# Two SwiGLU feed-forward layers of a hybrid encoder, their products rewritten as Strassen's seven

## The chip, the cores and the metric

The kernel runs on one core of one Trainium2 chip. The metric is the device time of one execution in microseconds (us), lower is better. TensorE multiplies, VectorE (DVE), ScalarE (ACT) and GpSimd (POOL) do the elementwise work, and SyncE (SP) issues every DMA of the program.

## The reference

Two layers work on 1024 tokens of 1024 channels in float32. Layer 0 mixes by a convolution and a recurrence, layer 1 by differential attention, and each is followed by a feed-forward part. `D_FF` is 2816, that is 22 tiles of 128 columns.

```python
def swiglu(x, w_gate, w_up, w_down):
    return (jax.nn.silu(x @ w_gate) * (x @ w_up)) @ w_down
...
for layer in range(DEPTH):            # 2
    y = conv_lru_mixer(...) if layer % 2 == 0 else diff_attention_mixer(...)
    x = layer_norm(DN_ALPHA * x + y, mix_ln_g[layer], mix_ln_b[layer])
    x = layer_norm(DN_ALPHA * x + swiglu(x, ffn_w_gate[layer], ffn_w_up[layer], ffn_w_down[layer]),
                   ffn_ln_g[layer], ffn_ln_b[layer])
```

## The kernel before

SBUF is 35 pages of 128x1024 float32 (`g`, given out by `alloc`, from the front of a queue into which released pages go at the end) beside two tiles `xt` that hold the transposed activations x^T. A page may be cut into two half pages (`halloc`). PSUM is eight banks of 128x512.

Every product is in the format float32r, on operands that are split first: `split` copies a number's high part with ScalarE and takes the rest with a VectorE subtraction whose two inputs are both in SBUF (or one in PSUM). `three` then issues three matmuls for one product of 128 x 128 by 128 x 512: high by high, high by low, low by high. So each tile product costs three matmuls of 512 columns, and each operand costs one ScalarE and one VectorE instruction.

The tokens are worked on in two halves, A (tokens 0 to 511) and B. In the feed-forward part a chunk is two column tiles: `ff_up` takes for each of them the gate's and the up projection's weights ("units", 128x1024, loaded and split whole) against the eight 128-row tiles of x^T, 24 matmuls for each of the two weights and each half; `ff_down` multiplies the chunk's activations, which stay in SBUF, with two units of the down projection, 48 matmuls for a half, into PSUM, and adds each bank to the residual page with a VectorE instruction. A chunk of one half is so 96 + 48 = 144 matmuls. The first chunks of half A (`ffn_lead`) are run earlier, beside other work, as cover: four of them (`lead0`) beside the VectorE-heavy convolution of half B in layer 0, ten (`lead1`) beside and after the attention of half B in layer 1. `mix` interleaves these: for each unit of time of the attention's products it lets `ratio2` = 1.5 units of feed-forward products run. `turn` transposes a half of x on TensorE, in 128x128 pieces, into `xt`.

The order of the instructions on each engine is not the order of the code. Class `Order` records every instruction and what it touches, prices each by a table of engine times, and gives each engine a list order by latest start; the order is fixed when the program is built. Every instruction is issued through one helper, so that nearly all rows of the profile carry one line, L378. They are told apart by engine, operation, tiles and shape.

Of the kernel before, what the change touches and what calls it, by code (L numbers as in the profile page):

```python
# [37 lines left out]
class _Fake:  # L38
    """Stands for every object of the tracer in the pass that only records the order of the units."""
# [20 lines left out]
class Page:  # L60
    """[128, 1024] of SBUF, or [128, 512]: a half of one of these or of a k tile of x^T."""
# [10 lines left out]
class Unit:  # L72
    """[128, 1024] of a weight: loaded, then split."""
# [9 lines left out]
class Order:  # L83
    """Records what the trace issues and what it touches, and gives each engine an order for it: of the
    instructions whose data is there, the one that the later ones wait for most urgently, on a model of the
    engines' times.  Only the order is taken from the model; Tile still derives every wait from the data."""
# [12 lines left out]
    # ------------------------------------------------------------- recording  # L99
# [83 lines left out]
    def price(self, eng, name, out, reads, a, k):  # L183
# [14 lines left out]
        if eng == "act":  # L198
            f = a[2] if name == "activation" else None
            fn = str(f).split(".")[-1] if f is not None else "Copy"  # L200
            src = reads[0]
# [29 lines left out]
    # ------------------------------------------------------------ scheduling  # L231
    def lag(self, p, o, raw):
        """time from the end of op p to the earliest start of op o, which depends on it."""
        if p.dma:
            return 1070 if o.eng == "pe" else 910
        if p.eng == o.eng:
            return (127 if p.eng == "dve" else 100 if p.eng in ("act", "pool") else 0) if raw else 0
        return {"pe": 197, "act": 140, "dve": 130, "pool": 75, "sp": 0}[p.eng] + (self.margin if o.eng == "pe" else 0)

    def solve(self):  # L240
# [6 lines left out]
        # latest starts, with the products back to back in the order of the trace  # L247
# [28 lines left out]
        # list scheduling  # L276
# [73 lines left out]
    def apply(self):  # L350
# [4 lines left out]
        # a page goes to its next user only when the one before has had it  # L355
# [29 lines left out]
class Core:  # L385
    """The engines, with every call recorded."""
# [6 lines left out]
# the order of layer 0's steps, up to the output projection of half A; the letters are those of layer0_in  # L393
# [3 lines left out]
class Trunk:  # L397
    def __init__(self, tc, io, order=None, lead0=4, lead1=10, ratio1=1.65, ratio2=1.5, pool_a=(13, 13, 12, 8), pool_b=9,
# [19 lines left out]
        self.ahead = 1  # L418

    # ---------------------------------------------------------------- memory  # L420
    def setup(self, sb, ps, dr):
# [8 lines left out]
        self.r_d = dr.tile([HALF, D], F32, name="r_d")  # L430
        self.SM = sb.tile([P, NSMALL], F32, name="SM")
# [10 lines left out]
        self.ring_x = deque()  # L442
        self.banks = deque(range(8))
# [6 lines left out]
    def ring(self, name, n, bufs):  # L450
        """n small columns out of a ring of bufs."""
# [13 lines left out]
    def halloc(self, r=False):  # L465
        """half a page, from a ring of these that takes in and gives back whole pages."""
# [7 lines left out]
    def pair(self):  # L474
        """[128, 2, 512]: half B of two k tiles of x^T while that holds nothing, or a page."""
        return self.ring_x.popleft() if self.ring_x else self.alloc(True)
# [5 lines left out]
    def part(self, p, b):  # L482
        """half b of a pair, or a half page."""
        return self.pr(p) if p.kind == "h" else self.two(p, True)[:, b, :]

    def lend(self):
        """half B of x^T as pages."""
        for i in range(8):
            t = (self.XTH, self.XTL)[i // 4][:, 2 * (i % 4):2 * (i % 4) + 2, HALF:]
            self.ring_x.append(Page(t, True, "x", i))  # L490

    def release(self, *pages):
        for p in pages:
            if p.kind == "g":
                self.free.append(p.idx)
            elif p.kind == "x":
                self.ring_x.append(p)
# [23 lines left out]
    # ----------------------------------------------------------------- units  # L521
# [7 lines left out]
    def load(self, key):  # L529
        u = Unit(self.alloc())  # L530
        src = self.unit_src(key)
        # the first units come in pieces, so that the products start with the first of these
# [14 lines left out]
    def split(self, hi, lo, src):  # L547
        """hi + lo = src exactly (24 bits), each in a form that float32r carries."""
# [3 lines left out]
    def prefetch(self, n=9999):  # L552
        """Loads ahead, as far as pages are free; three pages are kept for each unit until it is split."""
        if self.dry:
            return
        while (self.next_load < min(n, len(self.order)) and self.live < self.cap
# [35 lines left out]
    # ------------------------------------------------------------- products  # L592
    def three(self, out, ah, al, bh, bl, start, stop):
        """out += (ah + al)^T (bh + bl), without the product of the two low parts."""
# [5 lines left out]
    def colmul(self, bank, u, h):  # L600
        """bank[128 columns, 512 tokens] = unit^T x^T for half h."""
# [15 lines left out]
    # ----------------------------------------------------------- layer norm  # L617
# [5 lines left out]
    def layer_norm(self, r, g, b, spread=False, store=None, parts=1):  # L623
        """in place; the last steps are spread over ScalarE and GpSimd or done in parts, each stored at once."""
# [19 lines left out]
    def transpose_in(self, src, t):  # L644
        """x^T of token tile t, split, into XT."""
# [12 lines left out]
    # ------------------------------------------------------------ constants  # L658
    def constants(self):
# [11 lines left out]
        # per-channel vectors  # L671
# [8 lines left out]
    def mixer_constants(self):  # L680
        nc, io = self.nc, self.io
        # -8 softplus(-lambda), with softplus(y) = max(y, 0) + log1p(exp(-|y|)) and
        # log1p(e) = 2 atanh(e / (2 + e)) as a series that converges to float32 for e in [0, 1]
# [20 lines left out]
        # block-diagonal gate weights  # L704
# [11 lines left out]
    # -------------------------------------------------------------- layer 0  # L716
# [13 lines left out]
    def glu(self, i, h, bv, bg):  # L730
        """val * sigmoid(gate) of channel tile i; half B keeps the last 30 tokens of half A before its own."""
# [964 lines left out]
```

## Time and profile before

| | |
|---|---|
| three runs | 2483.09, 2487.78, 2487.95 us |
| median | 2487.78 us |
| the profiled execution, first to last instruction | 2481.7 us |
| mean granted TensorE clock | 0.972 of full speed |
| PE busy | 2351.1 us (95%), 10552 instructions |
| DVE busy | 1577.0 us (64%), 2235 |
| ACT busy | 874.4 us (35%), 1320 |
| POOL busy | 444.2 us (18%), 358 |
| DMA | 248.75 MB, mean 100 GB/s |

The profile gives no time of its own for the profiled execution beside its span; the three runs lie 1.4 to 6.2 us above this span, which is what lies around it. Shares are means over the whole program. A stage's limit is read from the stage.

### The profile page before, as it was taken

How to read it: one execution, taken by the hardware profiler on the slowest of the kernel's cores; microseconds unless marked ns; L12 is line 12 of the kernel's file. 1: busy time of each engine (PE TensorE's matmuls, PEld its weight loads, DVE VectorE, ACT ScalarE, POOL GpSimd, SP SyncE). 2: the span in 40 equal slices, each digit the busy share in tenths (PEclk: the TensorE clock that was granted, in tenths of full speed). 3: DMA queues.
4: the chain of work that ended last, by engine and by line, in shares of the span. 5: the costliest groups of instructions: out<-in, count | busy, mean ns of one | idle time of the engine just before them, and what ended most of it. 6: DMA issues, size and time to landing. Idle time of an engine off the chain costs nothing.

```text
span 2481.7 us, 27257 instructions
## 1 busy us (share of the span) xinstructions
PE 2351.1 (95%) x10552; PEld 1901.3 (77%) x10552; DVE 1577.0 (64%) x2235; ACT 874.4 (35%) x1320; POOL 444.2 (18%) x358
## 2 busy tenths in 40 slices
PE   9688988999999999999888789999999999999998
PEld 7466776888888888888666667777777888888887
DVE  8999998943333337464667677676766754644445
ACT  5245456321111113222334344555555522222221
POOL 4641334100000001012233334111111300100001
PEclk9888999999999999999989999999999999999999
DMA  5014223411111112335443356344333231233331
GB/s 185 9 43 149 72 68 111 147 54 45 48 46 44 50 51 77 96 105 176 133 146 115 113 173 203 114 136 133 120 110 111 87 122 64 102 94 102 95 101 60
DMA packets 95586, 248.75 MB, mean 100 GB/s; under 512 B 9952, under 2 KB 26592, under 8 KB 95456
## 3 DMA queue, kind: packets, MB, share of 16 engines
q1 hardware_dynamic: 95456, 247.00, 31.3%
q8 instruction: 83, 1.36, 0.2%
q14 instruction: 47, 0.39, 0.1%
HBM read 215.51 MB, written 31.46 MB: 100 GB/s over the span
## 4 chain that ended last, share of the span: by engine, by line
PE 71%; DMA 5%; DVE 4%; issue 1%; ACT 1%; POOL 0%; SPq 0%; DVEq 0%; POOLq 0%; ACTq 0%
PE PS L378 71%; DVE g L378 3%; DMA q_d<-g 3%; ACT g L378 1%; DVE SM L378 1%; DMA k_d<-g 1%; DMA g<-k_d 0%; DMA g<-q_d 0%; POOL g L378 0%; ACT xt L378 0%; DMA g<-in_qk 0%; POOL SM L378 0%; DMA v_d<-g 0%; SPq L378 0%; DVE PS L378 0%
## 5 line engine op out<-in xcount | busy, mean ns | idle before, releaser
L378 PE MATMUL PS<-xt,g 128*128 128x512 f32 x5776 | 1399.7, 397 | 25.0 <-DVE g L378 13.2
L378 PEld LDWEIGHTS PS<-xt,g 128*128 128x128 f32 x5776 | 1090.4, 191 | 269.0 <-DVE g L378 15.7
L378 PE MATMUL PS<-g,g 128*128 128x512 f32 (+2 forms) x2832 | 691.8, 391 | 81.7 <-DVE g L378 39.1
L378 DVE TENSOR_TENSOR g<-g,g 128x1024 fp32r<-128x1024 f32 (+2 forms) x523 | 547.8, 1061 | 294.9 <-ACT g L378 246.7
L378 ACT CAST g<-g 128x1024 fp32r<-128x1024 f32 (+1 forms) x435 | 394.4, 920 | 842.9 <-PE PS L378 388.9
L378 PEld LDWEIGHTS PS<-g,g 128*128 128x128 f32 x2832 | 520.5, 191 | 206.0 <-DVE g L378 43.6
L378 DVE TENSOR_TENSOR g<-g,PS 128x512 f32<-128x512 f32 x416 | 281.6, 685 | 387.0 <-PE PS L378 384.5
L378 POOL TENSOR_TENSOR g<-g,g 128x512 f32<-128x512 f32 (+9 forms) x182 | 292.2, 1607 | 658.6 <-ACT g L378 450.0
L378 PE MATMUL PS<-g,xt 128*128 128x512 f32 (+4 forms) x1176 | 259.4, 363 | 2.5 <-DVE g L378 2.0
L378 ACT ACTIVATE g<-PS,SM 128x512 f32<-128x512 f32 (+8 forms) x266 | 180.0, 687 | 186.9 <-PE PS L378 116.2
L378 PEld LDWEIGHTS PS<-g,xt 128*128 128x128 f32 (+1 forms) x1176 | 202.8, 189 | 50.7 <-issue 11.4
L378 POOL TENSOR_SCALAR SM<-SM 128x1 f32<-128x1 f32 x32 | 31.2, 975 | 1168.5 <-DVE SM L378 1167.7
L378 DVE SCALAR_TENSOR_TENSOR g<-g,SM,g 128x1024 f32<-128x1024 f32 (+9 forms) x215 | 235.5, 1105 | 5.0 <-POOL SM L378 2.2
L378 ACT ACTIVATE g<-PS 128x512 f32<-128x512 f32 (+1 forms) x152 | 83.7, 551 | 321.3 <-PE PS L378 313.0
L378 ACT ACTIVATE g<-g,SM 128x512 f32<-128x512 f32 (+9 forms) x100 | 71.3, 739 | 79.9 <-POOL g L378 51.5
L378 PE MATMUL PS<-SM,g 128*128 128x128 f32 (+1 forms) x608 | 91.1, 274 | 7.6 <-DVE g L378 5.2
L378 PEld LDWEIGHTS PS<-SM,g 128*128 128x128 f32 x608 | 77.2, 158 | 23.6 <-DVE g L378 7.5
L378 DVE TENSOR_REDUCE SM<-PS 128x2 f32<-128x256 f32 (+3 forms) x64 | 86.5, 1353 | 7.6 <-PE PS L378 6.1
L378 ACT CAST g<-PS 128x512 fp32r<-128x512 f32 (+1 forms) x96 | 52.5, 549 | 100.6 <-PE PS L378 100.5
L378 POOL TENSOR_TENSOR SM<-SM 128x1 f32<-128x1 f32 x96 | 68.1, 719 | 109.0 <-DVE SM L378 106.8
L378 DVE SCALAR_TENSOR_TENSOR g<-g,SM 128x512 f32<-128x512 f32 (+8 forms) x84 | 86.4, 1034 | 0.2
L378 DVE TENSOR_TENSOR g<-PS,g 128x512 fp32r<-128x512 f32 (+1 forms) x96 | 61.2, 640 | 34.3 <-ACT g L378 33.7
(44 smaller groups left out, 633.0 us busy)
## 6 DMA issues: line engine op xcount, KB each, us to landing
g<-in_up SPq DMA_DIRECT2D x72, 512.0 KB, 3.7
g<-in_gate SPq DMA_DIRECT2D x72, 512.0 KB, 3.7
g<-in_down SPq DMA_DIRECT2D x72, 512.0 KB, 3.6
g<-in_wout SPq DMA_DIRECT2D x32, 512.0 KB, 4.4
g<-in_win SPq DMA_DIRECT2D x22, 512.0 KB, 4.1
g<-k_d SPq DMA_DIRECT2D x34, 256.0 KB, 5.8
g<-in_v SPq DMA_DIRECT2D x16, 512.0 KB, 4.3
g<-in_qk SPq DMA_DIRECT2D x16, 512.0 KB, 5.3
```

The lines of the kernel that those rows point to most:

```text
L378: r = f(*a, **k)
```

## The change

For both layers the feed-forward part is rewritten. The gate and up products of a column tile for both token halves are one 2 by 2 block product (halves of the 1024 input channels, two token halves, gate against up), done with seven products of half the depth in place of eight: `ffn_lead` makes two of the seven (operands `a` and `b` of x, of half A alone) and writes the results to DRAM (`z_d`); `ffn_up` makes the other five, reads these back, forms both halves' activations and writes them to DRAM (`a_d`). `ffn_down` makes the down projection as seven products over halves of tokens, of the 22 row tiles and of the output channels, each of 11 steps of 12 matmuls, and adds each of the seven sums from PSUM into one or two of the four residual blocks. Sums of weights or activations that the seven need are made by GpSimd (`w_operand`, and the activation sums in `operands`) or by VectorE (weight sums in `ffn_down`, sums of x in `x_operand`). The residual goes through DRAM too (`x_d`). The cover is now `lead0` = `lead1` = 18 column tiles of two products each, with `ratio2` = 0.62.

```diff
-    def __init__(self, tc, io, order=None, lead0=4, lead1=10, ratio1=1.65, ratio2=1.5, ...
+    def __init__(self, tc, io, order=None, lead0=18, lead1=18, ratio1=1.65, ratio2=0.62, ...
...
+    def x_operand(self, name, u, a, b=None, op=ALU.add):
+        if b is not None:
+            s = self.halloc()
+            nc.vector.tensor_tensor(self.pg(s), a, b, op)
+            a = self.pg(s)
+        bk = self.bank()
+        for i in range(4):
+            nc.tensor.transpose(bk.ap[:, i * P:(i + 1) * P], a[:, i * P:(i + 1) * P], self.ident)
+        ...
+            self.split(hi, lo, b3[:, ks, :])
+
+    def operands_b(self):
+        self.xops = {n: [self.alloc(True) for _ in range(4)] for n in "efg"}
+        for u in range(4):
+            ...
+            self.x_operand("c", u, b22)
+            self.x_operand("d", u, b12, b22, ALU.subtract)
+            self.x_operand("e", u, b11, b22)
+            self.x_operand("f", u, b11, b12)
+            self.x_operand("g", u, b21, b22)
+            ...
+                nc.sync.dma_start(self.x_d[t], r)
+
+    def w_operand(self, a, b=None, op=ALU.add):
+        if b is not None:
+            s = self.halloc()
+            self.nc.gpsimd.tensor_tensor(self.pg(s), a, b, op)
+            a = self.pg(s)
+        p = self.pair()
+        self.split(self.part(p, 0), self.part(p, 1), a)
+
+    def product(self, bk, w, name, start=True, stop=True):
+        for k in range(4):
+            ...
+            self.three(bk.ap, wh[:, c], wl[:, c], xh, xl, start and k == 0, stop and k == 3)
+
+    def ffn_lead(self, l, fs, hook=None):
+        for f in fs:
+            pu, u1, u2 = self.raw("up", l, f)
+            w2, w4 = self.w_operand(u1, u2), self.w_operand(u2)
+            self.product(bk, w2, "a")
+            nc.scalar.copy(z0, bk.ap)
+            self.product(bk, w4, "b")
+            nc.vector.tensor_tensor(z1, bk.ap, z0, ALU.add)
+            nc.sync.dma_start(self.z_d[f], self.pg(z))
+
+    def ffn_up(self, l):
+        self.lend(0)
+        for f in range(NFF):
+            pg, g1, g2 = self.raw("gate", l, f)
+            pu, u1, u2 = self.raw("up", l, f)
+            nc.sync.dma_start(self.pg(z), self.z_d[f])
+            w3, w1 = self.w_operand(g1), self.w_operand(g1, u2)
+            self.product(bk, w3, "d")
+            nc.scalar.copy(v3, bk.ap)
+            nc.gpsimd.tensor_tensor(z0, v3, z0, ALU.subtract)
+            self.product(bk, w1, "e")
+            nc.vector.tensor_tensor(vu, bk.ap, z0, ALU.add)
+            self.product(bk, self.w_operand(g1, g2), "c")
+            nc.vector.tensor_tensor(v3, bk.ap, v3, ALU.add)
+            nc.scalar.activation(vs, v3, AF.Silu)
+            nc.gpsimd.tensor_tensor(vg, vu, v3, ALU.subtract)
+            nc.gpsimd.tensor_tensor(vg, vg, z1, ALU.add)
+            self.product(bk, self.w_operand(g2, u2, ALU.subtract), "g")
+            nc.vector.tensor_tensor(vg, bk.ap, vg, ALU.add)
+            nc.scalar.activation(vg, vg, AF.Silu)
+            nc.vector.tensor_tensor(aa, vg, z1, ALU.mult)
+            self.product(bk, self.w_operand(u1, g1, ALU.subtract), "f")
+            nc.vector.tensor_tensor(vu, bk.ap, vu, ALU.add)
+            nc.vector.tensor_tensor(ab, vu, vs, ALU.mult)
+            nc.sync.dma_start(self.a_d[f], self.pg(act))
+
+    def ffn_down(self, l, done, late):
+        plan = {3: (((0, 0),), None, ((0, 1), (1, 1)), S), 2: (((0, 1), (1, 1)), A, ((0, 0),), None),
+                5: (((0, 0), (1, 0)), A, ((1, 1),), None), 4: (((1, 1),), None, ((1, 0), (0, 0)), S),
+                1: (((0, 0), (1, 1)), A, ((0, 0), (1, 1)), A), 7: (((1, 0), (1, 1)), S, ((1, 0), (1, 1)), A),
+                6: (((0, 1), (0, 0)), S, ((0, 0), (0, 1)), A)}
+        def operands(m, f, get):
+            ls, lop, rs, rop = plan[m]
+            for i, (fh, dh) in enumerate(rs):
+                nc.sync.dma_start(self.two(p)[:, i, :], self.io["down"][l][f + n * fh][:, dh * HALF:(dh + 1) * HALF])
+            if rop:
+                nc.vector.tensor_tensor(self.two(p)[:, 0, :], self.two(p)[:, 0, :], self.two(p)[:, 1, :], rop)
+            self.split(self.part(right, 0), self.part(right, 1), self.two(p)[:, 0, :])
+            if lop:
+                nc.gpsimd.tensor_tensor(self.pg(s), src, act(f + n * ls[1][0], ls[1][1]), lop)
+            self.split(self.part(left, 0), self.part(left, 1), src)
+        ...
+        steps(3, al, range(n))
+        into(al, (r12, A), (r22, A))
+        ...
+        steps(7, be, range(n))
+        for t in range(4):
+            nc.vector.tensor_tensor(r11[t], r11[t], be[t].ap, A)
+            done(t)
+        steps(6, al, range(5), get)
+        ...
+        last = [operands(6, f, get) for f in range(n - 3, n)]
+        for t in range(4):
+            for i, (left, right) in enumerate(last):
+                step(al, left, right, t, False, i == 2)
+            nc.vector.tensor_tensor(r22[t], r22[t], al[t].ap, A)
+            done(t + 4)
```

Where the two programs differ most beside TensorE is GpSimd. In the kernel before, GpSimd does in the feed-forward part of layer 0 only two small instructions for each token tile's norm (`SM`) and the scaling of four residual pages:

```order
L378 TENSOR_SCALAR SM<-SM 128x1
L378 TENSOR_TENSOR SM<-SM 128x1
L378 TENSOR_SCALAR g_133_1576<-g_133_1576 128x1024
L378 TENSOR_SCALAR g_134_1578<-g_134_1578 128x1024
L378 TENSOR_SCALAR g_135_1580<-g_135_1580 128x1024
```

In the changed kernel the same engine has, in `ffn_up` of layer 0, these rows for one column tile (g_337 and g_338 are the gate and up weights of one column tile, g_335 and the half pages g_14, g_15 and g_317 the sums of the tile before it):

```order
L378 TENSOR_TENSOR g_315_3173<-g_337_3580,g_338_3582 128x512
L378 TENSOR_TENSOR g_335_3490<-g_317_3185,g_335_3490 128x512
L378 TENSOR_TENSOR g_315_3173<-g_337_3580 128x512
L378 TENSOR_TENSOR g_15_89<-g_14_88,g_317_3185 128x512
L378 TENSOR_TENSOR g_317_3185<-g_337_3580,g_338_3582 128x512
L378 TENSOR_TENSOR g_15_89<-g_15_89,g_335_3490 128x512
L378 TENSOR_TENSOR g_14_88<-g_338_3582,g_337_3580 128x512
```

Seven GpSimd additions for each of 22 column tiles, four for weights of the next tile between three for the results of the present one, stand where nothing stood.

On VectorE, in the feed-forward part of layer 0 before, additions of whole banks of `ff_down` (g_274 and so on, the residual pages, and PS, the bank) stand between splits of whole weight units:

```order
L378 SCALAR_TENSOR_TENSOR g_274_2919<-g_274_2919,PS 128x512
L378 SCALAR_TENSOR_TENSOR g_275_2921<-g_275_2921,PS 128x512 x2
L378 SCALAR_TENSOR_TENSOR g_276_2923<-g_276_2923,PS 128x512 x2
L378 SCALAR_TENSOR_TENSOR g_277_2925<-g_277_2925,PS 128x512 x2
L378 TENSOR_TENSOR g_340_3915<-g_333_3799,g_339_3914 128x1024
```

In the changed kernel, in `ffn_down` of layer 0 where product 4 passes into product 1, VectorE has for each step the sum of two weight halves (a page onto itself), the low part of it and the low part of the activation sum (both into `xt`, of which a half is lent for that), and the additions of the banks into the residual pages g_423 and g_424 between:

```order
L378 TENSOR_TENSOR g_423_5558<-g_423_5558,PS 128x512
L378 TENSOR_TENSOR g_507_6764<-g_507_6764 128x512
L378 TENSOR_TENSOR xt_74<-g_506_6743,xt_74 128x512
L378 TENSOR_TENSOR xt_74<-g_317_3185,xt_74 128x512
L378 TENSOR_TENSOR g_424_5560<-g_424_5560,PS 128x512
L378 TENSOR_TENSOR g_508_6785<-g_508_6785 128x512
L378 TENSOR_TENSOR g_511_6848<-g_511_6848 128x512
L378 TENSOR_TENSOR xt_74<-g_507_6764,xt_74 128x512
```

Three VectorE instructions with both inputs in SBUF now go with 12 matmuls, and g_317, read by the split of the left operand, is what GpSimd has summed just before. Over the whole program the 128x512 matmuls go from 9268 to 8476, the 128x128 transposes and small products of TensorE from 640 to 736, VectorE's 128x512 TENSOR_TENSOR instructions from 748 to 1438 and its 128x1024 ones from 303 to 87, GpSimd's 128x512 TENSOR_TENSOR instructions from 150 to 612, and ScalarE's table loads from 54 to 19.

## Rows read from the trace of the kernel before

**Rows 1.** Stages in windows: busy us and instructions by engine, clock, DMA.

```profile
266.00:490.00 224.00, 206.13 (x887) 166.91 (x886) 206.95 (x236) 117.44 (x154) 75.99 (x51) 0.96 0.30 101
490.00:1091.00 601.00, 600.87 (x2673) 496.74 (x2672) 257.13 (x338) 120.32 (x158) 16.23 (x18) 1.00 0.19 60
1091.00:1190.00 99.00, 98.32 (x448) 81.22 (x447) 53.69 (x74) 28.17 (x41) 19.70 (x16) 1.00 0.54 171
1190.00:1545.00 355.00, 306.01 (x1386) 240.46 (x1385) 241.87 (x472) 142.44 (x305) 119.51 (x99) 0.92 0.45 142
1545.00:1980.00 435.00, 430.96 (x2096) 335.17 (x2095) 308.14 (x479) 232.21 (x367) 79.70 (x71) 0.99 0.39 117
1980.00:2482.00 502.00, 493.37 (x2187) 408.15 (x2185) 257.74 (x319) 120.79 (x147) 20.90 (x22) 0.99 0.30 93
```

The columns are the window, its length, then PE, PEld, DVE, ACT and POOL busy us with their instructions, the granted clock, the DMA share and GB/s.

**Rows 2.** The same columns, inside the feed-forward part of layer 0.

```profile
558.00:930.00 372.00, 372.00 (x1636) 307.03 (x1635) 127.05 (x166) 59.24 (x77) 0.00 (x0) 1.00 0.15 48
```

**Rows 3.** Groups of 558 to 930 us: count, busy us, mean ns, idle before.

```profile
L378 DVE TENSOR_TENSOR g<-g,PS 128x512 f32<-128x512 f32 x104 | 70.9, 687 | 164.5 <-PE PS L378 164.1
L378 DVE TENSOR_TENSOR g<-g,g 128x1024 fp32r<-128x1024 f32 x32 | 39.2, 1224 | 70.2 <-ACT g L378 70.2
L378 DVE TENSOR_TENSOR g<-g,g 128x512 fp32r<-128x512 f32 x22 | 15.1, 687 | 4.1 <-ACT g L378 4.1
L378 ACT CAST g<-g 128x512 fp32r<-128x512 f32 x22 | 13.6, 620 | 70.7 <-DVE g L378 70.7
```

**Rows 4.** TensorE in order of time, transposes of one half: start, us, count.

```profile
974.63 3.65 PE L378 MATMUL PS<-SM,g 128*128 128x128 f32 x32
```

**Rows 5.** Waits of TensorE, 1190 to 1545 us: us, times, longest.

```profile
PE PS L378 <- DVE g L378: 32.6, 8, 8.8
PE PS L378 <- DMA g<-k_d: 9.4, 6, 3.6
```

**Rows 6.** VectorE in order of time, with GpSimd idle.

```profile
403.24 0.68 DVE L378 TENSOR_TENSOR g<-g,PS 128x512 f32<-128x512 f32 x1
403.84 2.49 DVE L378 SCALAR_TENSOR_TENSOR g<-g,g 128x512 f32<-128x512 f32 x4
```

**Rows 7.** GpSimd in order of time, with VectorE idle.

```profile
1503.02 1.28 POOL L378 TENSOR_TENSOR g<-g,g 128x512 f32<-128x512 f32 x1 [5.68 <-ACT g L378]
```

**Rows 8.** VectorE in order of time, both engines at work (convolution of layer 0).

```profile
113.28 1.70 DVE L378 SCALAR_TENSOR_TENSOR g<-g,SM 128x506 f32<-128x506 f32 x1
114.89 1.70 DVE L378 SCALAR_TENSOR_TENSOR g<-g,SM,g 128x505 f32<-128x505 f32 x1
```

**Rows 9.** GpSimd in order of time, the same stretch.

```profile
119.22 4.87 POOL L378 TENSOR_TENSOR g<-g,g 128x489 f32<-128x489 f32 x3
```

**Rows 10.** VectorE groups of the last 28 us (2454 to 2482 us).

```profile
L378 DVE SCALAR_TENSOR_TENSOR g<-g,SM,g 128x1024 f32<-128x1024 f32 x7 | 8.9, 1278 | 0.1
L378 DVE BATCH_NORM_STATS2 SM<-g 128x6 f32<-128x512 f32 x8 | 5.6, 694 | 0.3
L378 DVE BATCH_NORM_AGGREGATE SM<-SM 128x2 f32<-128x12 f32 x4 | 0.8, 208 | 0.1
```

**Rows 11.** TensorE in order of time, the same stretch.

```profile
2453.75 19.75 PE L378 MATMUL PS<-g,g 128*128 128x512 f32 x86
```

**Rows 12.** Windows of 10 us, columns as in rows 1.

```profile
20.00:30.00 10.00, 10.00 (x46) 8.29 (x45) 8.89 (x11) 8.11 (x9) 4.29 (x4) 1.00 1.01 328
200.00:210.00 10.00, 5.47 (x14) 3.79 (x15) 9.97 (x11) 8.13 (x11) 0.00 (x0) 0.52 0.47 168
1120.00:1130.00 10.00, 9.32 (x57) 7.95 (x56) 8.66 (x12) 7.32 (x12) 5.06 (x4) 1.00 1.06 408
1190.00:1200.00 10.00, 6.63 (x19) 4.30 (x19) 4.74 (x12) 3.00 (x6) 3.87 (x2) 0.66 0.44 159
```

## The prediction on record

> **What bounds the kernel now.** I read the stages in windows first, since shares over the whole span mix stages with different limits. The feed-forward part of layer 0 (490 to 1091 us) is TensorE alone: PE is busy 600.87 of 601 us at full clock, while DVE is busy 257 and POOL 16 [rows 1]. The same holds for the rest of layer 1's (1980 to 2482 us). Inside it 1636 matmuls take 372.00 us [rows 2], so a 512-column matmul costs 0.227 us, and DVE's idle time there is ended by PE [rows 3]. The attention of half B (1545 to 1980 us), filled with feed-forward products, is also bound by PE (430.96 of 435). The attention of half A (1190 to 1545 us) is what a stage looks like in which PE is not fed: busy 306.01 of 355 us, clock 0.92 [rows 1], and its longest waits are for DVE results (32.6 us) and DMA (9.4) [rows 5]. The stage with half B's convolution (266 to 490 us) is bound by DVE, 206.95 of 224 us [rows 1].
>
> So fewer matmuls pay at full price where PE is alone, and what other engines get on top counts where it reaches PE's time.
>
> **What is removed.** The program has 792 fewer 512-column matmuls: of each layer's 3168, seven eighths are left. At 0.227 us that is 180 us. It has 96 more 128x128 transposes; 32 take 3.65 us [rows 4], so 0.114 each, 11 us. Net: -169 us. That no product is left out of this is excluded by the program's count, 9268 to 8476.
>
> **Prices of the rest.** DVE instructions on 128x512 show 0.687 us each [rows 3], but their ends overlap: four take 2.49 us, so one follows another after 0.60 [rows 6]. A GpSimd addition with DVE idle takes 1.28 us [rows 7]. With both at work they hold each other up. In the convolution DVE instructions with two SBUF inputs take 1.70 us in place of 0.69 and start 1.61 us apart [rows 8], and three GpSimd additions take 4.87 us, 1.62 each [rows 9]. One addition and one such DVE instruction make a pair of 1.62 us, so each pair costs DVE 1.02 us of waiting. DVE instructions that read PSUM start 0.60 us apart between others [rows 6]; whether they wait too is not shown, so both ends are kept.
>
> **ffn_up.** A column tile is five products, 60 matmuls, 13.6 us of PE. DVE has 11 instructions (five splits, four bank reads, two products): 6.6 us, plus seven waits of 1.02, 13.7. GpSimd has seven additions, 7 x 1.62 = 11.3. ACT has eight instructions, under 0.7 us each (the split's 0.62 [rows 3] is the nearest), 5.6. DVE is at parity with PE only if every pair collides. Lower bound 0; upper bound PE at the pace of half A's attention, 306/355 = 0.86 [rows 1], 48 us a layer. It is nearest to the parity: I take 0.25 us a tile, 44 tiles, +10 (0 to +96). The weight sums stand one tile ahead on GpSimd, behind results of the present tile, so one late product delays the next tile's weights.
>
> **ffn_down.** 924 matmuls are 210 us of PE a layer. DVE: five products of 11 steps have three instructions a step and two have two, 209 in all, 125 us at 0.60; 48 additions of banks, 29 us; eight norms of two statistics, one aggregate and two long instructions, about 0.60 + 0.60 + 0.2 + 1.2 + 1.2 = 3.8 us each by their rows less the overlap [rows 10], 30 us. That is 184 us. 55 GpSimd additions add up to 55 x 1.02 = 56 us of waiting: 240. Between 184 and 240 PE's 210 is exceeded by 0 to 30 us a layer. The three last products (1, 7, 6) carry all the pairs of sums and the norms, so little can be worked ahead; I take the upper end, less 15 us in layer 0, whose last four norms lie beside layer 1's first products. At the very end, PE now gives 9 matmuls, 2.0 us, for a token tile where it gave 24 (86 took 19.75 [rows 11]: 5.5 us), and a tile's bank and norm take DVE 4.4, so norms queue: about 9 us, part of layer 1's 30. Total 15 + 30, +45 (+9 to +60).
>
> **Half B's attention, thinner cover.** Before, 3168 matmuls less the some 2155 of the 2187 instructions after 1980 us [rows 1] were in it, 1013, 230 us; with 32 transposes (4) the attention itself needs PE for 431 - 234 = 197 us. Now 432 matmuls (98 us) and 32 transposes are its cover: 299 us of PE. DVE: of 308 us, 7.0 chunks of six unit splits at 1.224 and twelve at 0.687 [rows 3], 15.6 us each, go: 199 left, and 18 x 3 + 12 instructions at 0.687 come, 45: 244 of 299, 82%, where it was 71%; in half A's it is 68% and PE is idle all the same. PE at 0.99 gives +3, at half A's 0.86 +48. I take the middle, +26 (0 to +48).
>
> **Half B's convolution.** Its cover was 528 matmuls (120 us), now 432 (98). DVE loses 4 x 15.6 = 62 us, gets 18 x 3 + 12 instructions, 45, and waits for 18 GpSimd additions, up to 18. DVE, which bounds the stage, is so about where it was, and the 22 us of products taken out here are not gained: 0 to +22, taken +12.
>
> **Hand-over to ffn_up.** `operands_b` is 36 DVE instructions (22 us at 0.60) behind half B's last four norms (15); PE has 96 matmuls and 80 transposes beside it, 31 us. Short by 6: +5 a layer, +10 (0 to +40, the 20 us after the norms uncovered, twice).
>
> **DMA.** The first two products of `ffn_down` load 8 residual pages, 22 activation pages and 33 half units: 24.4 MB in 60 us of PE, 407 GB/s. The fastest windows moved 408 and 328 GB/s [rows 12]. A part is loaded ahead: +5 (0 to +28, at 328).
>
> Losses: 10 + 45 + 26 + 12 + 10 + 5 = 108. The sum is 2481.7 - 169 + 108 = 2421 us in the profile's span; the median of the runs lies 6.1 us above this span, so **2427 us**.
>
> **A rule weighed.** The row says 1.62 us for a pair, less than 1.28 + 0.60 = 1.88. The Trainium skill ("SBUF — State Buffer", Who interferes with whom) says that a VectorE instruction with two SBUF inputs and a GpSimd one that reads SBUF exclude each other for the whole instruction, the second blocking fully, and that one with at most one SBUF input does not contend. By it the pair would be 1.88 us; the trace shows the blocking, at the smaller price, so the sum goes by 1.62.
>
> **Rivals.**
> *Everything is hidden*: the splits and sums work ahead and only the end's norms show. For it: ACT and DMA have room, and DVE is busy 43% of layer 0's feed-forward part [rows 1]. 2487.8 - 169 + 9 = 2328.
> *Pairs at their full price*: 1.88 us, and nothing overlaps. `ffn_up`: 7 x 1.88 + 4 x 0.60 = 15.56 us a tile against 13.62, 85 for 44; `ffn_down`: 184 + 55 x 1.28 = 254 against 210, twice 44 less 15, 73; the four other losses 53. 2487.8 - 169 + 211 = 2530. Against it: the pair's measured 1.62. It makes the kernel slower where the two parts lose over 116 us in place of my 55. This is what the rule of the Trainium skill's page above comes to when no other work fits into the blocked time.
> *TensorE starved, at a lower clock (slower)*: DVE and GpSimd wait for each other in line, a split comes late, PE stops, and the clock falls. The rows show it: where PE was busy 5.47 of 10 us the granted clock was 0.52, near the lower level of 1.2 GHz, and 0.66 where it was busy 6.63 [rows 12]. The feed-forward products outside the attentions and half B's attention are 2 x 2340 x 0.227 + 299 = 1361 us of PE. At efficiency e they cost 1361 (1/e - 1) more; the 169 us are gone at e = 0.89. At half A's 0.86 it is 218 us, with the convolution's 12: 2487.8 - 169 + 230 = 2549. Against it: in steady parts weights can be split several products ahead.
> *DMA late in ffn_down*: the +28 in place of +5, 2450. For it: SP issues in line, and the last store of activations stands ahead of loads.
>
> **Numbers.** Chances: mine 0.60, all hidden 0.13, DMA 0.07, pairs at full price 0.07, starved 0.13. The first three are faster by more than 0.2% (5 us, about what a measurement of this kernel can tell): 0.80. Of the slower two some end within 5 us: same 0.03, slower 0.17. My own case, with its terms not all at one end together, reaches from 2350 to 2480; the range takes in most of the hidden case and the near end of the slower ones: 2335 to 2500.
>
> **What would show it.** Right: 8476 matmuls still at 0.227 us; `ffn_up` near 300 us a layer with DVE over 85% busy and DVE instructions of 1.7 us; `ffn_down` 210 to 245 with DVE near full in its last three products; half B's attention near 325 us. Wrong: PE under 0.89 busy over the feed-forward parts, clock under 0.95 there (starved); DVE under 75% with PE full (hidden). I would be wrong most easily by the waits of pairs, since no stage of before has both engines this busy beside a full TensorE.

## The result, and the profile after

The changed kernel takes 2530.81 us (median of four runs, 2524.22 to 2533.04) against 2485.7 us for the kernel before in the same runs: a ratio of 1.0177, 95% interval 1.0158 to 1.0196. It is slower by 45 us where 61 us faster was forecast, and lies above the range.

The first lines of its page give the engines' busy time and the chain of work that ended last.

```profile
PE 2259.6 (89%) x9856; PEld 1786.1 (71%) x9856; DVE 1912.2 (76%) x2725; ACT 985.8 (39%) x1733; POOL 1146.4 (45%) x836
...
PE 35%; DVE 22%; POOL 17%; DMA 11%; issue 11%; ACT 4%; SPq 1%; POOLq 0%; DVEq 0%; ACTq 0%
```

The saving is there: 696 TensorE instructions fewer (792 matmuls less 96 transposes). But TensorE's busy time fell only from 2351.1 to 2259.6 us, and not by the 169 us that these instructions cost at full clock. Of the difference to a span of 2530.3 us, 140 us came back as waiting and 78 as longer busy time, beside a mean granted clock of 0.945 where it was 0.972. The stages in windows, with the columns of [rows 1], say where:

```profile
266.00:490.00 224.00, 191.95 (x781) 150.09 (x780) 194.51 (x223) 97.60 (x148) 96.93 (x67) 0.92 0.33 115
490.00:540.00 50.00, 45.76 (x227) 36.14 (x226) 48.86 (x75) 22.31 (x50) 27.66 (x21) 0.97 0.70 237
540.00:870.00 330.00, 309.20 (x1311) 244.22 (x1310) 199.64 (x247) 102.77 (x175) 223.99 (x149) 0.99 0.44 155
870.00:930.00 60.00, 43.75 (x170) 34.62 (x169) 37.92 (x56) 22.95 (x40) 16.71 (x13) 0.86 0.74 273
930.00:1054.00 124.00, 124.00 (x549) 102.70 (x548) 114.46 (x156) 50.92 (x88) 44.13 (x33) 1.00 0.56 178
1054.00:1121.00 67.00, 56.41 (x243) 45.99 (x242) 64.91 (x82) 23.91 (x37) 34.35 (x25) 0.90 0.41 143
1121.00:1566.00 445.00, 394.71 (x1778) 314.11 (x1778) 289.02 (x546) 163.66 (x339) 134.57 (x113) 0.93 0.47 147
1566.00:1893.00 327.00, 308.95 (x1514) 230.89 (x1513) 245.27 (x416) 169.05 (x322) 101.96 (x90) 0.96 0.44 139
1893.00:1945.00 52.00, 41.58 (x204) 33.35 (x203) 50.19 (x71) 22.20 (x49) 33.23 (x26) 0.87 0.62 211
...
2480.00:2530.00 50.00, 31.07 (x118) 23.85 (x116) 46.19 (x62) 6.25 (x11) 20.94 (x21) 0.80 0.35 126
```

Half B's attention is as forecast, 327 us for 325. The middle of `ffn_down` (930 to 1054 us) is TensorE alone, 124.00 of 124: there nothing is lost. The three stretches around it lose. In `ffn_up` (540 to 870) TensorE stands for 21 of 330 us at nearly full clock, while VectorE is busy only 60% and GpSimd 68%: no engine is full. At the start of `ffn_down` (870 to 930) TensorE is busy 43.75 of 60 us. At the program's end VectorE is busy 46.19 of 50.

**`ffn_up`: a line that waits for itself.** The stores of activations, one a column tile, give the pace: first and last start us of 18 stores.

```profile
L378 SPq DMA_DIRECT2D a_d<-g x18: 320/327/327, 600.2 to 859.4; - x18
```

That is 259.2 / 17 = 15.25 us a tile, where TensorE needs 13.6. GpSimd in order of time, one tile and the beginning of the next:

```profile
675.69 4.60 POOL L378 TENSOR_TENSOR g<-g,g 128x512 f32<-128x512 f32 x3 [2.55 <-DVE g L378]
680.26 1.73 POOL L378 TENSOR_TENSOR g<-g 128x512 f32<-128x512 f32 x1
684.05 4.30 POOL L378 TENSOR_TENSOR g<-g,g 128x512 f32<-128x512 f32 x3 [2.06 <-DVE g L378]
690.90 1.67 POOL L378 TENSOR_TENSOR g<-g,g 128x512 f32<-128x512 f32 x1 [2.55 <-DVE g L378]
```

Seven additions take 10.6 us, and two waits for VectorE, 2.06 and 2.55 us, make it 15.2, tile after tile. GpSimd works in line. The wait of 2.06 is the result sum `vg = vu - v3` that waits for VectorE's `v3`; the weight sums of the next tile stand behind it. The wait of 2.55 is such a weight sum, `u1 - g1`: the half page that it writes comes from a ring of ten halves and was read last by VectorE's product `ab` of the present tile, which waits for TensorE's last product, which waits for splits of earlier weight sums. This closes a loop. TensorE, VectorE and ACT all wait inside it (waits of 600 to 800 us: us, times, longest):

```profile
ACT xt L378 <- POOL g L378: 103.9, 53, 2.8
DVE xt L378 <- ACT xt L378: 83.4, 40, 3.2
POOL g L378 <- DVE g L378: 62.5, 27, 2.6
...
PE PS L378 <- ACT xt L378: 8.7, 14, 0.7
```

**The start of `ffn_down`.** TensorE in order of time, its two long gaps in layer 0, and two windows around them:

```profile
880.12 8.23 PE L378 MATMUL PS<-xt 128*128 128x512 f32 x24 [6.47 <-ACT xt L378]
897.37 5.41 PE L378 MATMUL PS<-xt 128*128 128x512 f32 x12 [9.02 <-ACT xt L378]
```

```profile
860.00:885.00 25.00, 15.24 (x48) 11.57 (x49) 19.33 (x24) 6.31 (x11) 6.37 (x5) 0.80 1.00 373
885.00:895.00 10.00, 3.35 (x14) 2.41 (x12) 7.04 (x12) 5.26 (x10) 0.00 (x0) 0.84 1.03 404
```

In these windows the DMA engines are full, at 373 to 404 GB/s. Whether bytes were too many, or loads began too late, a profile alone doesn't say.

### The profile page after: what moved, and what is told of

It is laid out like the page before. It is cut to its first block, busy times and chain, and to the rows that moved or that the text cites. A ratio compares the mean times of both kernels' runs of the same rounds, so it can differ in the third digit from the quotient of the medians.

```text
span 2530.3 us, 28521 instructions
## 1 busy us (share of the span) xinstructions
PE 2259.6 (89%) x9856; PEld 1786.1 (71%) x9856; DVE 1912.2 (76%) x2725; ACT 985.8 (39%) x1733; POOL 1146.4 (45%) x836
## 4 chain that ended last, share of the span: by engine, by line
PE 35%; DVE 22%; POOL 17%; DMA 11%; issue 11%; ACT 4%; SPq 1%; POOLq 0%; DVEq 0%; ACTq 0%
PE PS L378 35%; DVE g L378 18%; POOL g L378 16%; DMA q_d<-g 4%; DVE xt L378 2%; ACT g L378 2%; DVE SM L378 2%; ACT xt L378 1%; DMA g<-in_down 1%; DMA g<-a_d 1%; POOL SM L378 1%; DMA k_d<-g 1%; DMA g<-k_d 1%; SPq L378 1%; DMA g<-in_up 1%
## 5 line engine op out<-in xcount | busy, mean ns | idle before, releaser
L378 POOL TENSOR_TENSOR g<-g,g 128x512 f32<-128x512 f32 (+6 forms) x507 | 763.2, 1516 | 947.6 <-DVE g L378 370.0
L378 PE MATMUL PS<-g,xt 128*128 128x512 f32 (+3 forms) x2768 | 669.6, 386 | 47.5 <-ACT xt L378 23.2
L378 DVE TENSOR_TENSOR xt<-g,xt 128x512 fp32r<-128x512 f32 x532 | 459.4, 885 | 311.7 <-ACT xt L378 305.8
L378 PE MATMUL PS<-xt,g 128*128 128x512 f32 x2416 | 639.5, 415 | 50.8 <-DVE g L378 29.4
L378 PEld LDWEIGHTS PS<-g,xt 128*128 128x128 f32 (+1 forms) x2768 | 502.7, 191 | 188.5 <-ACT xt L378 38.0
L378 PE MATMUL PS<-xt 128*128 128x512 f32 x2232 | 599.0, 396 | 33.9 <-ACT xt L378 33.9
L378 PEld LDWEIGHTS PS<-xt,g 128*128 128x128 f32 x2416 | 470.4, 199 | 171.7 <-DVE g L378 40.2
L378 ACT CAST xt<-g 128x512 fp32r<-128x512 f32 x532 | 314.2, 619 | 583.1 <-POOL g L378 365.3
L378 PEld LDWEIGHTS PS<-xt 128*128 128x128 f32 x2232 | 426.1, 191 | 128.1 <-ACT xt L378 36.7
L378 DVE TENSOR_TENSOR g<-g,g 128x512 f32<-128x512 f32 (+2 forms) x451 | 396.7, 899 | 98.9 <-DMA q_d<-g 50.0
```

The costliest lines, as they stand in the source:

```text
L378: r = f(*a, **k)
```

## The experiments

For all runs of one group the kernel before ran on the same chip; the groups ran on different chips, where its median was 2482.45 to 2488.01 us. The table gives us between the starts of the same matmuls, counted along TensorE's list (9856 in every kernel; a few stand in another order, so 1 to 2 us may shift between neighbours). It is worked out from the traces: `up` is nearly all of `ffn_up` (1286 and 1291 of its 1320 matmuls in each layer; at 0.227 us 292 and 293), `start` the next 191 and 203 (43 and 46), `end` the last 281 and 115 of `ffn_down`, A and B the two attentions, `tail` from the last matmul's start to the end.

```
                 up0  start0  end0    A     B   up1  start1  end1  tail
changed kernel   319    71     76    430   342  319    75     34    16
larger ring      292    80     76    426   342  293    82     34    18
results on DVE   291    67     76    424   347  293    68     33    18
up on DVE        291    66     77    428   344  293    67     32    18
down on DVE      319    71     66    421   346  319    75     26    24
both on DVE      291    66     66    424   345  293    67     26    23
half loads       291    66     66    422   342  293    67     26    23
late residual    291    49     71    426   341  293    53     26    28
held pages       291    69     66    424   344  293    69     26    23
both start edits 291    44     72    424   346  293    47     26    28
ring and late    292    64     81    423   344  293    64     41    16
```

**Larger ring.** In `ffn`, on the changed kernel:

```
-        self.trim({False: 5, True: 0})
+        self.trim({False: 8, True: 0})
```

> The ring of bf16 half pages in the up-projection holds 16 halves instead of 10; nothing else changes. Queue theory: a column tile takes 15.2 us because GpSimd, which works in line, has the weight sum u1-g1 of the next tile waiting about 2.5 us for a half page that the present tile's last product still reads; with more halves this wait goes, the a_d stores of the up-projection stand 13.6 to 14.2 us apart, and the whole time falls by 40 to 70 us, to 2460 to 2490. Lock theory (the pairs of VectorE and GpSimd operations that lengthen each other set the pace by themselves): stores still 15.0 to 15.2 us apart, time 2525 to 2533.

Measured 2486.77 us, ratio to before 0.9996 (0.9978 to 1.0014): 44 us of the loss gone with one number. The stores, and the waits of GpSimd and ACT in 600 to 800 us:

```profile
L378 SPq DMA_DIRECT2D a_d<-g x18: 319/326/327, 596.5 to 835.7; - x18
```

```profile
ACT xt L378 <- POOL g L378: 55.1, 42, 2.1
POOL g L378 <- DVE g L378: 39.5, 28, 2.2
```

239.2 / 17 = 14.07 us a tile. (The half pages hold float32, 128x512 f32 in the rows, and not bf16 as the expectation says.) No addition was moved, so the pairs are all left, and TensorE is full (200.00 of 200 us in 600 to 800). So the pairs by themselves did not set the 15.25; the loop through the ring did. The stores are still 0.5 us a tile slower than TensorE's 13.6: from one to the next it does 62 matmuls, where a tile has 60, so it works ahead on later tiles and loses nothing over these 22. The Trainium skill ("Perfetto Trace Analysis", Optimization Strategy) says that a gap that repeats on the engine that should be full can mean too little SBUF for the next tile, and the trace agrees: six more halves took 1.2 us off every tile. The start of `ffn_down` got 9 and 7 us longer. The ring took three pages, and the runs on the start of `ffn_down` further down bear on that.

**Result sums on VectorE.** The three sums of results go to VectorE, the ring stays at ten:

```
-            nc.gpsimd.tensor_tensor(z0, v3, z0, ALU.subtract)
+            nc.vector.tensor_tensor(z0, v3, z0, ALU.subtract)
...
-            nc.gpsimd.tensor_tensor(vg, vu, v3, ALU.subtract)
-            nc.gpsimd.tensor_tensor(vg, vg, z1, ALU.add)
+            nc.vector.tensor_tensor(vg, vu, v3, ALU.subtract)
+            nc.vector.tensor_tensor(vg, vg, z1, ALU.add)
```

> The three result sums of the up-projection that stood on GpSimd are on VectorE; the four weight sums stay on GpSimd. Queue theory: GpSimd has only 4 operations of 1.3 to 1.7 us a tile and never waits behind a result sum, so stores stand 13.6 us apart, time 2460 to 2470. Lock theory: four pairs of seven are left, stores 14.0 to 14.4 us apart, time 2485 to 2500.

**All sums of `ffn_up` on VectorE.** The four weight sums too (`w_operand` takes `eng=nc.vector`).

> No GpSimd operation in the up-projection at all: weight sums and result sums on VectorE. VectorE then has about 18 operations of 0.60 us a tile, 10.8 us of TensorE's 13.6. Queue theory and lock theory both: 13.6 us apart, time 2455 to 2470; it gives the floor of the up-projection for the other two. Rival: VectorE's own line becomes the loop (a split that waits stands in front of a result that TensorE's banks wait for), then 14 to 16 us apart and no gain.

Measured 2461.5 us (0.9899, 0.984 to 0.9958) and 2458.64 us (0.9887, 0.9847 to 0.9928). The stores of both, the first row with the four weight sums left on GpSimd:

```profile
L378 SPq DMA_DIRECT2D a_d<-g x18: 319/326/327, 594.6 to 825.5; - x18
```

```profile
L378 SPq DMA_DIRECT2D a_d<-g x18: 320/326/327, 588.4 to 819.3; - x18
```

13.58 us a tile in both: TensorE's own pace. Four pairs of seven cost nothing once no weight sum stands behind a result sum. The queue theory holds.

**Activation sums of `ffn_down` on VectorE.** In `operands`, `ffn_up` as it was:

```
-                nc.gpsimd.tensor_tensor(self.pg(s), src, act(f + n * ls[1][0], ls[1][1]), lop)
+                nc.vector.tensor_tensor(self.pg(s), src, act(f + n * ls[1][0], ls[1][1]), lop)
```

> The activation sums of the down-projection are on VectorE rather than GpSimd; the up-projection is as it was. Lock theory: VectorE loses the waits of its pairs in the last stretch of the down-projection, which ends 10 to 12 us sooner in each layer, time 2505 to 2515. Rival: the end of the down-projection is set by the norms and the last result sums, which are VectorE's own; the added operations take what the pairs give back, time 2525 to 2535. The start of the down-projection (87 us for 66 us of products) should not move if it is the transfers that it waits for.

Measured 2514.26 us (1.0111, 1.0065 to 1.0158), 16.6 better. By the table both theories have their part: layer 0's end is 10 us shorter, as the lock theory said; layer 1's gives 8 us on TensorE and takes 8 in the tail, as its rival said. Another 9 us appear in half A's attention (430 to 421), where no edit was made but the recorded order differs; later edits give between 2 and 9 there, and what makes them is open.

**Both together.**

> All sums of both feed-forward products on VectorE, in the up-projection (as in the run without GpSimd there, 2458.6 us) and in the down-projection (as in the run that had only that, 16.5 us less). If the two gains are separate things: 2440 to 2446. If VectorE, now the only engine for sums, fills up in the down-projection once the up-projection feeds it sooner: 2455 to 2462. The start of each down-projection still takes some 85 us for 66 us of products.

Measured 2446.29 us (0.9843, 0.9808 to 0.9879), at the edge of the 2440 to 2446 of two separate gains: 12 of the 16.6 us add up. The start takes 66 and 67 us as before.

**Half loads.** `act` loads the half that is asked for:

```
+            if (f, h) not in got:
+                got.add((f, h))
+                nc.sync.dma_start(self.pg(acts[f])[:, half], self.a_d[f][:, half])
```

> As the run before it, but the down-projection loads only the half of an activation page that a product needs, when it needs it: 2.9 MB fewer in each layer's first two products. Transfer theory (the first products of the down-projection wait for bytes: 17 MB in 45 us at 378 GB/s): 2.9 MB is 7.6 us a layer, 12 to 16 us in all, 2426 to 2432. Page theory (they wait for SBUF pages that are given back late, whatever the bytes): under 4 us, about as the run before it.

Measured 2444.07 us (0.9834, 0.9779 to 0.989), start unchanged. This tells nothing on bytes, for the edit did not do what it says. SP in order of time, without it and with it, the first two steps of product 3:

```profile
808.72 1.11 SPq L378 DMA_DIRECT2D g<-in_down  x2
809.89 2.35 SPq L378 DMA_DIRECT2D g<-a_d  x2
```

```profile
805.80 0.95 SPq L378 DMA_DIRECT2D g<-in_down  x2
806.80 2.09 SPq L378 DMA_DIRECT2D g<-a_d  x4
```

Four halves in place of two pages: the recorded order put the second half's load, which waits for no page, right behind the first's.

**Late residual.** On the version with both sums on VectorE, the eight pages are taken and loaded six steps into product 2:

```
-        for t in range(8):
-            self.r[t] = self.alloc()
-            nc.sync.dma_start(self.pg(self.r[t]), self.x_d[t])
...
         steps(3, al, range(n))
+        steps(2, be, range(6))
+        for t in range(8):
+            self.r[t] = self.alloc()
+            nc.sync.dma_start(self.pg(self.r[t]), self.x_d[t])
         into(al, (r12, A), (r22, A))
-        steps(2, be, range(n))
+        steps(2, be, range(6, n))
```

> As the first run of this group, but the eight pages of the residual (4.2 MB a layer) are taken and loaded six steps into product 2 rather than ahead of product 3. The eight pages are then free for product 3's operands while the up-projection still runs. Page theory: product 3's loads start 25 us earlier and the gap of some 18 us in TensorE goes, 25 to 36 us in all, 2405 to 2418. Transfer theory: the same bytes fall into the same stretch, the gap is moved to product 2; 0 to 10 us, 2430 to 2442. Rival (slower): the sums into the residual come late, product 5 waits for its banks, 2445 to 2455.

**Held pages.** The same, but eight pages are set aside until then:

```
+        hold = [self.alloc() for _ in range(8)]
         steps(3, al, range(n))
         steps(2, be, range(6))
+        self.release(*hold)
```

> As the run with the late residual (2420.5 us), but eight SBUF pages are set aside, unused, while product 3 and the first six steps of product 2 are issued; only then are they free, and the residual is taken and loaded as in that run. The bytes of that run stand where they stood, the pages are missing as they were before. Page theory: the loads of product 3 start late again, the gap in TensorE of 12 us in each layer is back, 2438 to 2450. Byte theory (what helped was that 4.2 MB of the residual no longer went ahead of product 3): 2418 to 2426.

Measured 2420.51 us (0.9739, 0.9708 to 0.9771) and 2446.73 us (0.9851, 0.9792 to 0.9911; its two runs 2440.84 and 2452.62). The late residual gives 25.8 us, within the 25 to 36 of the page theory though 2.5 above the time it named, and holding the pages takes them back. The longest gap of TensorE in layer 0's start without the edit, with the late residual, and with pages held, one row each:

```profile
857.51 4.87 PE L378 MATMUL PS<-xt 128*128 128x512 f32 x12 [12.05 <-ACT xt L378]
```

```profile
855.88 49.50 PE L378 MATMUL PS<-xt 128*128 128x512 f32 x211 [3.58 <-ACT xt L378]
```

```profile
860.79 4.95 PE L378 MATMUL PS<-xt 128*128 128x512 f32 x12 [12.45 <-ACT xt L378]
```

The loads of `in_down` issued in 700 to 825 us, in the same order of kernels:

```profile
L378 SPq DMA_DIRECT2D g<-in_down x11: 328/382/735, 805.9 to 824.9; - x11
```

```profile
L378 SPq DMA_DIRECT2D g<-in_down x19: 327/425/971, 776.2 to 823.9; - x19
```

```profile
L378 SPq DMA_DIRECT2D g<-in_down x15: 328/390/1242, 781.5 to 824.6; - x15
```

The loads of the residual, in the same order once more:

```profile
L378 SPq DMA_DIRECT2D g<-x_d x8: 319/320/640, 778.7 to 797.3; - x8
```

```profile
L378 SPq DMA_DIRECT2D g<-x_d x8: 319/319/376, 815.0 to 850.6; - x8
```

```profile
L378 SPq DMA_DIRECT2D g<-x_d x8: 319/320/436, 853.0 to 884.9; - x8
```

With the pages free, loads begin 30 us earlier, beside `ffn_up`. With the pages held, the first ones begin early too, but fewer come by 825 us (15 for 19, and 11 without the edit), and the whole gap is back. Yet the residual's bytes come latest there, from 853.0 us on, while with the late residual their loads start at 815.0 us, beside the operands of product 3, and only the wait of 3.58 us above follows. So the cause is pages and not the residual's bytes: without the edit eight pages were filled with the residual from 778.7 us on, for sums that come after product 3. How the missing pages make the gap is argued and not shown: the loads that the first products needed came in one burst, and the DMA engines are full then (1.00 and 1.03 in the windows of the changed kernel above); but they are as full from 825 to 840 us with the late residual, at 403 GB/s.

**Both start edits.**

> Both edits. Page theory and transfer theory together: the gap at the start of each down-projection, some 18 us, is gone, 2400 to 2412. If only one of the two causes is real, the time of the better of the two runs before it, within 4 us.

Measured 2417.71 us (0.9728, 0.9694 to 0.9762). This is 2.8 better than the late residual alone, so within the 4 us expected if only one of the two causes is real, and above the 2400 to 2412 of both. The start is at TensorE's pace, 44 and 47 us.

```profile
830.00:874.00 44.00, 43.65 (x191) 35.36 (x190) 28.55 (x47) 16.12 (x28) 0.00 (x0) 1.00 0.96 360
```

**Lead sums on VectorE.** In `ffn_lead`, on top of that, `self.w_operand(u1, u2, eng=nc.vector)`:

> As the run with both edits of the start (2417.7 us), and the one sum of weights of each tile that is worked ahead beside the second half's convolution and attention is on VectorE: no GpSimd operation is left in the feed-forward part. Pair theory (a GpSimd addition makes a VectorE operation with two SBUF inputs wait 1.02 us, and the convolution's stage is bound by VectorE): 18 sums there cost VectorE 0.60 each in place of 1.02, the stage gets 5 to 8 us shorter, 2408 to 2414. Rival (GpSimd's additions fall into time in which VectorE reads PSUM or stands, and cost it nothing): VectorE gets 11 us more to do, 2422 to 2432.

Measured 2405.5 us (0.9685, 0.9669 to 0.9701), the fastest here: 77 us faster than before in the same group, some 125 faster than the change as it was made. By matmul count 4 us come ahead of the conv stage, 7 in it and at the hand-over. VectorE has 18 operations more in that part and still ends sooner, which is the pair theory's sign, with somewhat more than its 8 us. The recorded order differs too, so that the pairs make all of the 12 us is not shown.

**Fourteen tiles ahead.** `lead0=14` for 18, on top of that.

> As the run before it, with 14 in place of 18 tiles beside layer 0's second convolution; the other four come after it, before the up-projection. If the convolution's stage is bound by VectorE, it gets 4 x 4 x 0.6 = 10 us shorter and the products moved cost TensorE 96 x 0.227 = 22 us after it, less the few us in which TensorE waits for the operand sums there: 6 to 12 us slower. If the products are what the stage is waiting for, 22 us go and 22 come: the same within 4 us.

Measured 2423.37 us (0.9758, 0.9733 to 0.9783), 18 us slower, more than the 6 to 12 expected. In the profiled executions 11 us are lost before `ffn_up`, 3 at the start of `ffn_down` and 7 in half B's attention, which has no edit. So the products moved cost more after the convolution than beside it.

**Ring and late residual alone.** The changed kernel, all sums on GpSimd, with the first edit and the late residual:

> The changed kernel with two small edits alone and all sums left on GpSimd: 16 half pages in place of 10 in the up-projection (that alone: 2486.8 us), and the residual's pages taken and loaded in product 2. If the stall in the up-projection and the one at the start of the down-projection are separate, the second gives 2 x 17 us also here: 2448 to 2458. If the larger ring (three pages more) has taken what the late residual frees: 2465 to 2480.

Measured 2465.01 us (0.9926, 0.9906 to 0.9946), at the lower edge of the 2465 to 2480 expected if the ring has taken what the late residual frees. `ffn_up` runs at its pace (292), but the start keeps 64 us of 80, where with both sums on VectorE the late residual left 49. Three pages more for the ring are three fewer for the loads: the two cures draw on one store of pages.

## Why the prediction was wrong

Its terms, with what the traces show. "Measured" is the time of a stretch less its matmuls at 0.227 us.

| step | said | measured |
|---|---|---|
| net work taken from PE | -169 | -169 (696 instructions fewer; 549 in 124.0 us, 0.226 each) |
| `ffn_up` | +10 | +53 (27 and 26) |
| start of `ffn_down` | +5 | +56 (28 and 29) |
| end of `ffn_down`, norms | +45 | about +28 (12 and 24, less the tail of 8 before) |
| half B's attention | +26 | +28 (327 less 299) |
| half A's attention | 0 | +6 |
| half B's convolution and what leads to it | +12 | about +30 |
| hand-over | +10 | +15 (50 less 45.76; 52 less 41.58) |

The convolution's row is layer 0's last norm of half B, whose aggregate starts at 501.4 us and before at 493.2, with 96 matmuls (22 us) fewer beside it. The tail before is 2481.7 less the end of [rows 11]. Half A's row is from the first store of `q_d` to the reload of the residual, 354.5 us before and 361.0 after. The losses add up to 216, and 2481.7 - 169 + 216 = 2529 us stands against the span of 2530.3. The forecast's last term, 6.1 us from the span to a run's time, was too large as well: each run on record lies about 1.8 us above its own span (2532.05 for 2530.3), and the rest was the spread between executions.

**The step that failed first** is "DVE is at parity with PE only if every pair collides ... I take 0.25 us a tile". Its price for GpSimd was near (1.62 us an addition; they took 1.3 to 1.7). VectorE's was too high: its splits took 1.03 us on the mean and not 1.70, and it was busy 60% of `ffn_up`, where over 85% had been named as the sign of being right. So parity was not reached, and yet the stage was slow, because the step compared sums of busy time, engine by engine, and none was over 13.7. The pace, 15.25 us a tile, was set by a loop through two engines and a ring of buffers: the larger ring gave 14.07, and the result sums on VectorE 13.58. The prediction saw half of it ("weight sums stand ... behind results of the present tile, so one late product delays the next tile's weights") and gave it no price; the ring it did not count.

**The second** is "8 residual pages, 22 activation pages and 33 half units: 24.4 MB in 60 us ... A part is loaded ahead: +5". The sum of bytes was right and the upper bound, 28 for both layers, rested on a rate. What counted was when pages came free: the part loaded ahead was the residual, the one thing not needed yet. Freeing its pages took the start from 66 and 67 us to 49 and 53, and holding them empty brought 69 and 69 back.

**The third** is the convolution's cover, whose upper bound of 22 was passed. Layer 0's norms of half A end later (two of its last aggregates at 279.9 and 281.1 us, before at 264.4 and 272.4), and 11 of these us went with the lead sums. The rest is not settled.

What held: the work removed, half B's attention, the hand-over, and the mechanism at the end of `ffn_down`; there the size was too high, since products 2 to 4 ran at full pace.

**The rivals.** *Pairs at their full price* gave 2530 us and 15.56 us a tile, near the 2530.8 and 15.25 that came, and for a wrong reason: with all seven pairs left, the larger ring runs at 14.07. *TensorE starved, at a lower clock* had the first half of what took place in `ffn_up`: engines waited for each other in line, splits came late and TensorE stopped, though for 0.7 us at the longest in 600 to 800 us, and the granted clock stayed at 0.99. Its second half, the lower clock, is seen at the start and the end of `ffn_down` (0.80 to 0.90). *DMA late* named the right place, and not the pages.

## What to carry to other kernels

Busy times that each fit below the bound do not show that a loop fits: follow one tile through every engine that works in line and every ring of buffers, and add up the waits that stand between a buffer's last reader and its next writer. At the border of two stages, ask which pages are held by data that is not needed yet; a load that is early for nothing makes a needed one late. An engine with lower rates that helps out saves nothing when the fuller engine still has time: here VectorE took over GpSimd's sums in the feed-forward part, group by group, and in no run did that make the kernel slower.

## What the hardware showed

VectorE operations with both inputs in SBUF are lengthened beside GpSimd, those with one input in PSUM are not. Groups of 600 to 800 us (count, busy us, mean ns, idle before): the changed kernel, the larger ring, and no GpSimd operation at all.

```profile
L378 DVE TENSOR_TENSOR xt<-g,xt 128x512 fp32r<-128x512 f32 x66 | 68.0, 1031 | 85.1 <-ACT xt L378 83.4
L378 DVE TENSOR_TENSOR g<-PS,g 128x512 f32<-128x512 f32 x52 | 34.3, 679 | 0.0
```

```profile
L378 DVE TENSOR_TENSOR xt<-g,xt 128x512 fp32r<-128x512 f32 x73 | 97.2, 1332 | 14.6 <-ACT xt L378 8.5
L378 DVE TENSOR_TENSOR g<-PS,g 128x512 f32<-128x512 f32 x58 | 38.4, 681 | 16.6 <-POOL g L378 16.6
```

```profile
L378 DVE TENSOR_TENSOR xt<-g,xt 128x512 fp32r<-128x512 f32 x73 | 49.0, 687 | 1.3
```

The split takes 0.687 us alone, 1.03 beside a GpSimd that is busy 69% and 1.33 beside one that is busy 79%; the read of a bank stays at 0.68. This settles what the prediction had kept open (whether reads of PSUM wait too). The Trainium skill ("SBUF — State Buffer", Who interferes with whom) says the same of instructions with at most one SBUF input, and the trace agrees. With both engines 79% busy TensorE was still full in the larger ring's run: there the longer operations cost TensorE no time (292 us for 291), though the stores came 0.5 us a tile later than without them.
